# New places in SBUF for the split weight tiles of a decoder block: hi, lo and activation tiles all at 0 modulo 512 bytes

## The chip, the cores and the metric

The kernel runs on one core of one Trainium2 chip. The time is device microseconds (us) of one execution, the median of several runs. A nanosecond is written ns.

## The reference, cut to what matters

One decoder block on 256 tokens of 2048 float32 channels (depth 1): a combined input projection, a gated linear attention branch and a forgetting attention branch, their merge and output projection, LayerNorm, a gated MLP with a width-3 causal convolution, LayerNorm, and a gated embedding.

```python
proj = x @ w_in                                        # 2048 x 13336
y_gla = gla(...) @ w_branch_gla;  y_fox = fox(...) @ w_branch_fox
merged = sigmoid(ma) * y_gla + sigmoid(mb) * y_fox
x = layer_norm(ALPHA * x + merged @ w_out)
h = gelu(causal_dwconv(x @ w_gate)) * (x @ w_up)       # 2048 x 5632, twice
x = layer_norm(ALPHA * x + h @ w_down)                 # 5632 x 2048
x = x + sigmoid(x @ w_ple_gate) * (p @ w_ple_proj)
```

## The kernel before, in words

**Splitting.** All large products are made from float32r operands. Each weight chunk `raw` (128 partitions by 1024 float32) is loaded by a DMA, ScalarE (ACT) copies it to `hi` in float32r (L77, called from L101), and VectorE (DVE) writes `lo = raw - hi` (L103). Activations are split likewise and kept side by side: a tile such as `xT` or `x1T` has, for each of four k tiles, 256 columns of high part and 256 columns of low part.

**Units.** The weights come as 284 units of two chunks (`hi` and `lo` for each). `prep()` loads and splits one unit, `unit()` hands one out and keeps the preparation up to three units ahead.

**Weight-stationary products** (`w_unit`, L169 and L171): for each of the 16 k tiles of a unit one matmul with 128 columns of `hi` as stationary operand and the activation's 512 columns moving, and one with the same columns of `lo` and the activation's 256 high columns moving. These are the q, k, gate, up and branch products. I call the two matmuls a pair, and the eight pairs that use one `hi` tile and its `lo` tile a half-unit.

**Token-stationary products** (`x_mm`, L213): 128 columns of the activation are stationary and 512 columns of `hi` or `lo` move (v, r, the output projection `wo`, the down projection `dn`, the last gate `pg`, and `pp`, the embedding's projection, whose split weights `pw` and activations `pTs` both lie in tiles of the S8 pool).

**The first stage** (`fv`, L320) is token-stationary too, with rows of 1048 columns (`fvhi`, `fvlo`) cut in 352, 352 and 344 columns. After it, ACT copies its results out of PSUM (`smtok`, `fv`), TensorE (PE) transposes `smtok`, the gates are started (`gSt`, `psg` L396), and the first weight-stationary unit (`psfq`) follows.

**The core's other matmul groups** that the prediction names: `go` (L636), whose moving tile `vs` lies in the S8 pool and whose stationary tiles `ath`/`atl` lie in the pool of 2 KB scratch tiles.

**Places.** Tile pools give each tag a number of equal places in SBUF, as large as the tag's largest tile, and a tile takes a place at its first write. Before the change `hi` and `lo` share their tags with `fvhi` and `fvlo` (six places each, 1048 x 4 = 4192 bytes, so that the next place starts 96 bytes further modulo 512). The start of each tile per partition, modulo 512 bytes, as the built program has it:

| tiles | before | after |
|---|---|---|
| `hi`, six places | 32, 128, 224, 320, 416, 0 | 0 |
| the `lo` that goes with it | 96, 192, 288, 384, 480, 64 | 0 |
| S8 tiles (activations `xT`, `x1T`, `x2T`, `oT`, `ofT`, `mT`, `hT0` to `hT9`; `vs`, `pw`, `pTs`) | 160 | 0 |
| `hT10` | 416 | 128 |
| scratch tiles `ath`, `atl` | 160 | 384 |
| `fvhi`, `fvlo` | as `hi`, `lo` | 0 |

A k tile's 128 stationary columns are 512 bytes and an activation's k tile 2048 bytes, so steps inside a tile leave the value modulo 512 as it is, except in the first stage, whose chunks start 1408 and 2816 bytes into a row.

**What sets the order.** DMA issues on SyncE's queue (SP) stand in the program's order; the other engines' instructions are ordered by a scheduler when the program is built, which takes free places into account. In that order each engine's queue is strict.

Of the kernel before, what the change touches and what calls it, by code (L numbers as in the profile page):

```python
# [9 lines left out]
F32 = mybir.dt.float32  # L10
F32R = mybir.dt.float32r
# [8 lines left out]
P = 128  # L20
# [12 lines left out]
NS = 1048  # L33
# [4 lines left out]
AFF_DVE = (0, 2)  # L38
LN_ORDER = (1, 0, 3, 2)
GROWS = 96  # L40

OFF = dict(gq=0, gk=1024, gv=2048, gr=4096, glr=6144, fq=6160, fk=7184, fv=8208,
           ff=9232, ma=9240, mb=11288)
# [3 lines left out]
def tile_block(ctx: ExitStack, tc: tile.TileContext, wu, wfv, wpp, xT_in, x_in, pT_in, wlr,  # L47
# [1 line left out]
    nc = tc.nc  # L49

    cst = ctx.enter_context(tc.tile_pool(name="cst", bufs=1))
    ring = ctx.enter_context(tc.tile_pool(name="ring", bufs=6))
    big = ctx.enter_context(tc.tile_pool(name="big", bufs=15))
    sm = ctx.enter_context(tc.tile_pool(name="sm", bufs=2))
    early = ctx.enter_context(ExitStack())
    ec = early.enter_context(tc.tile_pool(name="ec", bufs=1))
# [1 line left out]
    pmx = ctx.enter_context(tc.tile_pool(name="pmx", bufs=2, space=PSUM))  # L58
    dr = ctx.enter_context(tc.tile_pool(name="dr", bufs=1, space=DRAM))

    def s8(shape, dt=F32, name=None):
        return big.tile(shape, dt, tag="S8", name=name)

    def t1(name):
        return sm.tile([P, 256], F32, tag="t1", bufs=6, name=name)
# [10 lines left out]
    def copy(o, i, scale=1.0):  # L76
        nc.scalar.activation(o, i, AF.Copy, bias=0.0, scale=scale)  # L77
# [15 lines left out]
    def prep():  # L93
        u = n_prep[0]
        n_prep[0] += 1
        his, los = [], []
        for h in range(2):
            raw = ring.tile([P, 1024], F32, tag="raw", bufs=4, name=f"raw{u}_{h}")
            nc.sync.dma_start(raw, wu[u, :, h * 1024:(h + 1) * 1024])
            hi = ring.tile([P, 1024], F32R, tag="hi", name=f"hi{u}_{h}")  # L100
            copy(hi, raw)  # L101
            lo = ring.tile([P, 1024], F32R, tag="lo", name=f"lo{u}_{h}")
            nc.vector.tensor_tensor(lo, raw, hi.bitcast(F32), ALU.subtract)  # L103
            his.append(hi)
            los.append(lo)
        ready[u] = (his, los)
# [4 lines left out]
    def unit():  # L111
        u = n_used[0]
        n_used[0] += 1
        while n_prep[0] < min(NU, u + 3):
            prep()
        return ready.pop(u)


    xT = [s8([P, 4, 512], F32R, name=f"xT{g}") for g in range(4)]

    def load_x(g, k0, k1, step=2):
# [6 lines left out]
                                    xT[g][:, e, 0:256].bitcast(F32), ALU.subtract)  # L128


    chn = cst.tile([P, chan.shape[1]], F32, name="chn")
    c_blr, c_bf = 0, 8
    c_g1, c_b1, c_g2, c_b2 = 9, 25, 41, 57
    c_cw = 73
    c_cb = c_cw + 3 * NF
    ident = cst.tile([P, P], F32, name="ident")
    mask = ec.tile([P, 8, 256], U8, name="mask")
    cmask = ec.tile([P, 256], F32, name="cmask")
    gnb = ec.tile([P, 512], F32, name="gnb")
    reset = ec.tile([P, 256], F32, name="reset")  # L140
    ones = ec.tile([P, P], F32R, name="ones")
    gSt = ec.tile([P, 256], F32R, name="gSt")
    mhalf = cst.tile([P, 1], F32, name="mhalf")
    nc.gpsimd.memset(mhalf, -0.5)
    nc.gpsimd.memset(reset, 1.0)
    copy(ones, reset[:, 1:2].broadcast_to([P, P]))
# [2 lines left out]
    def load_consts():  # L149
        nc.sync.dma_start(ident, ident_in)  # L150
        nc.sync.dma_start(chn, chan)
        nc.sync.dma_start(cmask, cmask_in)
# [128 lines left out]


    fv = s8([P, 2, 1024], name="fv")
    fch = ((0, 352), (352, 352), (704, 344))
    fbk = [[mmtile(f"fv_{t}{c}") for c in range(3)] for t in range(2)]

    def fv_prep(u, hs=(0, 1), his=None, los=None):
        his, los = his or [], los or []
        for h in hs:
            raw = ring.tile([P, NS], F32, tag="raw", bufs=4, name=f"fvraw{u}_{h}")  # L290
            hi = ring.tile([P, NS], F32R, tag="hi", name=f"fvhi{u}_{h}")
            lo = ring.tile([P, NS], F32R, tag="lo", name=f"fvlo{u}_{h}")
            for o, n in fch if u == 0 else ((0, NS),):
                e = slice(o, o + n)
                nc.sync.dma_start(raw[:, e], wfv[u, :, h, e])
                copy(hi[:, e], raw[:, e])
                nc.vector.tensor_tensor(lo[:, e], raw[:, e], hi[:, e].bitcast(F32), ALU.subtract)
            his.append(hi)
            los.append(lo)
        return his, los  # L300

    load_x(0, 0, 1, 1)
    f0 = fv_prep(0, (0,))
    load_x(0, 1, 2, 1)
    fvu = [fv_prep(0, (1,), *f0)]
    load_x(0, 2, 4)
    fvu.append(fv_prep(1))
    load_x(1, 0, 4)
    for u in range(8):
        hi, lo = fvu[u]  # L310
        for j in range(2):
            kt = 2 * u + j
            a = xT[kt // 4][:, kt % 4, :]
            for cs in ((0,), (1,), (2,)) if u == 0 else ((0, 1, 2),):
                for t in range(2):
                    ah, al = a[:, t * P:t * P + P], a[:, 256 + t * P:256 + t * P + P]
                    for i, (w, x) in enumerate(((hi[j], ah), (lo[j], ah), (hi[j], al))):
                        for c in cs:
                            o, n = fch[c]
# [9 lines left out]
        elif u == 4:  # L329
            load_consts()  # L330
    wraw = s8([GROWS, 1024], name="wraw")
    nc.gpsimd.memset(wraw, 0.0)
    for i in range(3):
        nc.sync.dma_start(wraw[32 * i:32 * i + 16], wlr)
    wS = s8([GROWS, 1024], F32R, name="wS")
    copy(wS, wraw)
# [3 lines left out]
    for t in range(2):  # L340
# [4 lines left out]
        copy(tk[:, P:P + FH], fbk[t][2][:, 336:344])  # L345
        nc.tensor.transpose(smp[:GROWS, t * P:t * P + P], tk[:, 0:GROWS], ident)
        nc.tensor.transpose(smp[:FH, 256 + t * P:256 + t * P + P], tk[:, P:P + FH], ident)
    for t in range(2):
        for c, (o, n) in enumerate(fch):
            n = min(n, 1024 - o)  # L350
# [4 lines left out]
    cd = dr.tile([FH, 256], F32, name="cd")  # L355
    gS = gSt[:GROWS]
    copy(gS, smp[:GROWS, 0:256])
    nc.vector.tensor_tensor(gS[32:48], smp[32:48, 0:256], gS[32:48].bitcast(F32), ALU.subtract)
# [137 lines left out]
    for nm, dst, sc in (("fq", fq, P ** -0.5), ("fk", fk, 1.0)):  # L496
        if nm == "fk":
            mixers.append(fox_gen())
        for n in range(8):
            hi, lo = unit()  # L500
# [8 lines left out]
    for nm, dst, sc in (("q", gq, 1.0 / 16.0), ("k", gk, 1.0)):  # L509
        for n in range(8):  # L510
            hi, lo = unit()
            ps = mmtile(f"ps{nm}{n}")
            w_unit(ps, hi, lo, xT, range(16), True, True)
            h, c = n // 2, n % 2
# [163 lines left out]
    for n in range(32):  # L678
        hi, lo = unit()
# [14 lines left out]
    for n in range(16):  # L694
        hi, lo = unit()
# [270 lines left out]
    for n in range(NF):  # L966
# [17 lines left out]
        u = t1("up")  # L984
# [140 lines left out]
```

## Time and profile before

| | |
|---|---|
| median of 3 runs | 1709.56 us (1709.23 to 1710.12) |
| span of the profiled execution, first to last instruction | 1706.3 us |
| PE busy, share of the span | 1698.7 us, 100% |
| DVE, ACT, POOL busy | 64%, 49%, 2% |
| DMA traffic | 330.22 MB, mean 194 GB/s |
| TensorE's granted clock | 1.00 |

The profiled execution is known by its span; the runs' median is 3.3 us longer, which is what lies around the first and last instruction. A matmul's row has its start, and a duration that includes the time until its last column has left the array; the next matmul starts earlier than that, so what one costs is read from the distance between starts (or from a piece of the chain of waits, which is counted from start to start), not from the duration. PEld is the weight load, which runs beside the matmul ahead of it. Of a view's columns, "x24" is the number of instructions in a row or group, and what stands in brackets is idle time before it and what ended it.

### The profile page before, as it was taken

To read this page: it belongs to the slowest core of one execution; us is meant where nothing else is said; L and a number is where in the kernel's file an instruction comes from. 1 tells how busy PE (TensorE), PEld (TensorE's weight loads), DVE (VectorE), ACT (ScalarE), POOL (GpSimd) and SP (SyncE) were. 2 spreads that over 40 slices of the span, in tenths; PEclk is the share of its full clock that TensorE was granted. 3 is DMA by queue.
4 is the path that set the end of the run, shared out by engine and by line. 5 is a ranking of instruction groups with operands and counts; after the bars stand their busy time and mean duration, and the time that the engine had idled before them with its cause. 6 is when DMAs were issued, how large, how long until landed. Compare 5 with 4: busy or idle time off the path is not lost.

```text
span 1706.3 us, 23834 instructions
## 1 busy us (share of the span) xinstructions
PE 1698.7 (100%) x9035; PEld 1456.3 (85%) x9035; DVE 1098.4 (64%) x1588; ACT 833.5 (49%) x1200; POOL 36.3 (2%) x123
## 2 busy tenths in 40 slices
PE   9999999999999999999999999999999999999998
PEld 8888888888888888888788888888888888888787
DVE  6666668758756557774687776666666644544674
ACT  5745445445555544443364444454445433334633
POOL 0000000000000000000010000000000000000000
PEclk9999999999999999999999999999999999999999
DMA  9754455555554555557655665555555575555454
GB/s 309 233 190 167 163 185 173 181 177 173 176 177 166 171 187 187 191 189 283 205 175 196 210 212 194 187 187 191 187 189 188 190 287 188 188 193 198 156 175 171
DMA packets 91427, 330.22 MB, mean 194 GB/s; under 512 B 10232, under 2 KB 11904, under 8 KB 89904
## 3 DMA queue, kind: packets, MB, share of 16 engines
q1 hardware_dynamic: 90528, 324.51, 56.1%
q0 software_dynamic: 784, 4.20, 0.7%
q8 instruction: 70, 1.15, 0.3%
q14 instruction: 45, 0.37, 0.1%
HBM read 323.42 MB, written 5.25 MB: 193 GB/s over the span
## 4 chain that ended last, share of the span: by engine, by line
PE 98%; DVE 1%; DMA 0%; ACT 0%; SPq 0%; issue 0%; POOL 0%
PE dn L213 14%; PE psu L169 9%; PE psg L169 9%; PE psm L169 7%; PE gr L213 5%; PE gv L213 5%; PE wo L213 5%; PE pg L213 5%; PE psu L171 5%; PE psg L171 5%; PE psm L171 4%; PE psa L169 3%; PE fv L320 2%; PE psa L171 2%; PE psfq L169 2%; PE psq L169 2%
## 5 line engine op out<-in xcount | busy, mean ns | idle before, releaser
L103 DVE TENSOR_TENSOR lo<-raw,hi 128x1024 fp32r<-128x1024 f32 x568 | 694.1, 1224 | 517.4 <-ACT hi L77 516.3
L77 ACT ACTIVATE hi<-raw 128x1024 fp32r<-128x1024 f32 x568 | 601.6, 1060 | 745.9 <-issue 277.2
L169 PE MATMUL psu<-x1T,hi 128*128 128x512 f32 x688 | 242.3, 393 | 0.0
L169 PE MATMUL psg<-x1T,hi 128*128 128x512 f32 x672 | 236.7, 393 | 0.0
L213 PE MATMUL dn<-hi,hT 128*128 128x512 f32 x704 | 193.2, 394 | 0.0
L171 PE MATMUL psu<-x1T,lo 128*128 128x256 f32 x688 | 192.8, 280 | 0.0
L171 PE MATMUL psg<-x1T,lo 128*128 128x256 f32 x672 | 188.4, 280 | 0.0
L169 PE MATMUL psm<-xT,hi 128*128 128x512 f32 x512 | 180.1, 395 | 0.0
L213 PEld LDWEIGHTS dn<-hi,hT 128*128 128x128 f32 x704 | 132.1, 188 | 30.9
L169 PEld LDWEIGHTS psu<-x1T,hi 128*128 128x128 f32 x688 | 129.1, 188 | 29.6
L169 PEld LDWEIGHTS psg<-x1T,hi 128*128 128x128 f32 x672 | 126.1, 188 | 28.9
L171 PE MATMUL psm<-xT,lo 128*128 128x256 f32 x512 | 143.3, 280 | 0.0
L171 PEld LDWEIGHTS psu<-x1T,lo 128*128 128x128 f32 x688 | 129.6, 188 | 0.0
L171 PEld LDWEIGHTS psg<-x1T,lo 128*128 128x128 f32 x672 | 126.6, 188 | 0.0
L169 PEld LDWEIGHTS psm<-xT,hi 128*128 128x128 f32 x512 | 96.3, 188 | 21.7
L213 PE MATMUL dn<-lo,hT 128*128 128x512 f32 x352 | 111.8, 395 | 0.0
L171 PEld LDWEIGHTS psm<-xT,lo 128*128 128x128 f32 x512 | 96.5, 188 | 0.2
L169 PE MATMUL psa<-oT,hi 128*128 128x512 f32 x256 | 90.1, 393 | 0.0
L213 PEld LDWEIGHTS dn<-lo,hT 128*128 128x128 f32 x352 | 66.1, 188 | 15.5
L213 PE MATMUL gv<-hi,xT 128*128 128x512 f32 x256 | 73.6, 399 | 0.0
L213 PE MATMUL gr<-hi,xT 128*128 128x512 f32 x256 | 73.5, 399 | 0.0
L213 PE MATMUL wo<-hi,mT 128*128 128x512 f32 x256 | 71.7, 395 | 0.0
(247 smaller groups left out, 2435.4 us busy)
## 6 DMA issues: line engine op xcount, KB each, us to landing
raw<-in_wu_dram SPq DMA_DIRECT2D x568, 512.0 KB, 3.6
fvraw<-in_wfv_dram SPq DMA_DIRECT2D x14, 524.0 KB, 6.3
lnb<-in_lng_dram SPq DMA_DIRECT2D x4, 1024.0 KB, 12.1
z<-in_x_dram SPq DMA_DIRECT2D x2, 1024.0 KB, 7.6
praw<-in_wpp_dram SPq DMA_DIRECT2D x4, 512.0 KB, 3.8
x1d<-z POOLq DMA_DIRECT2D x2, 1024.0 KB, 5.3
z<-x1d SPq DMA_DIRECT2D x2, 1024.0 KB, 7.6
xraw<-in_xT_dram SPq DMA_DIRECT2D x7, 256.0 KB, 7.1
```

Of the source, the lines that this page charges most:

```text
L77: nc.scalar.activation(o, i, AF.Copy, bias=0.0, scale=scale)
L103: nc.vector.tensor_tensor(lo, raw, hi.bitcast(F32), ALU.subtract)
L169: nc.tensor.matmul(ps, lhsT=hi[i // 8 if hoff == 0 else 0][:, w0 % 1024:w0 % 1024 + P], rhs=a[:, kt % 4, :], start=first and i == 0, stop= ...
L171: nc.tensor.matmul(ps[:, 256:512], lhsT=lo[i // 8 if hoff == 0 else 0][:, w0 % 1024:w0 % 1024 + P], rhs=a[:, kt % 4, 0:256], start=False, ...
L213: nc.tensor.matmul(bs[j][:, 0:m], lhsT=x, rhs=v[:, o:o + m], start=first and i == 0, stop=last and i == 2)
L320: nc.tensor.matmul(fbk[t][c][:, 0:n], lhsT=x, rhs=w[:, o:o + n], start=kt == 0 and i == 0, stop=kt == 15 and i == 2)
```

## The change

`hi` and `lo` get a pool of their own (`wide`) with places of 4096 bytes, laid out ahead of the others. `fvhi` and `fvlo` are no longer in the `hi` and `lo` rings but take tiles of the S8 pool (15 places), which `s8()` now always asks for at 2048 columns and cuts to shape. `raw` keeps four places of 4192 bytes. A tile `pad` of 88 columns and the moved constants bring the first place to 0 modulo 512. No instruction is added or taken away.

```diff
+PAD = 88
+S8W = 2048
+W4 = 1024
...
-    ring = ctx.enter_context(tc.tile_pool(name="ring", bufs=6))
+    wide = ctx.enter_context(tc.tile_pool(name="wide", bufs=6))
     big = ctx.enter_context(tc.tile_pool(name="big", bufs=15))
+    ring = ctx.enter_context(tc.tile_pool(name="ring", bufs=4))
...
+    pad = cst.tile([P, PAD], F32, name="pad")
...
     def s8(shape, dt=F32, name=None):
-        return big.tile(shape, dt, tag="S8", name=name)
+        t = big.tile([P, S8W], dt, tag="S8", name=name)
...
+    def w_tile(tag, dt, name):
+        return wide.tile([P, W4], dt, tag=tag, name=name)[:, 0:1024]
...
-            hi = ring.tile([P, 1024], F32R, tag="hi", name=f"hi{u}_{h}")
+            hi = w_tile("hi", F32R, f"hi{u}_{h}")
...
-            lo = ring.tile([P, 1024], F32R, tag="lo", name=f"lo{u}_{h}")
+            lo = w_tile("lo", F32R, f"lo{u}_{h}")
...
-            hi = ring.tile([P, NS], F32R, tag="hi", name=f"fvhi{u}_{h}")
-            lo = ring.tile([P, NS], F32R, tag="lo", name=f"fvlo{u}_{h}")
+            hi = s8([P, NS], F32R, name=f"fvhi{u}_{h}")
+            lo = s8([P, NS], F32R, name=f"fvlo{u}_{h}")
```

The order of instructions is the same on SP and POOL, and on the other engines everywhere but between the first stage and the first units. ACT at the end of the first stage, before (`wS` is a small split weight, `hi_0_622` and `hi_1_628` are the first unit's two chunks):

```order
L77 ACTIVATE wS<-wraw 96x1024
L77 ACTIVATE hi_0_622<-raw_0_620 128x1024
L77 ACTIVATE hi_1_628<-raw_1_626 128x1024
L77 ACTIVATE smtok<-fv_113 128x16
L77 ACTIVATE smtok<-fv_113 128x16 x2
L77 ACTIVATE smtok<-fv_113 128x8
L77 ACTIVATE fv<-fv_111 128x352
L77 ACTIVATE fv<-fv_112 128x352
```

ACT at the same place now, from the second token tile's copies on (`wS` stands seven rows ahead, right before the first `fv`; `hi_0_626` and `hi_1_632` are the first unit's chunks):

```order
L96 ACTIVATE fv<-fv_118 128x352
L96 ACTIVATE smtok<-fv_120 128x16
L96 ACTIVATE smtok<-fv_120 128x16 x2
L96 ACTIVATE smtok<-fv_120 128x8
L96 ACTIVATE fv<-fv_119 128x352
L96 ACTIVATE fv<-fv_120 128x320
L96 ACTIVATE gSt<-smp 96x256
L96 ACTIVATE hi_0_626<-raw_0_624 128x1024
L96 ACTIVATE hi_1_632<-raw_1_630 128x1024
```

The first unit's two copies have moved from ahead of the copies out of PSUM to behind them and behind `gSt`; the two subtractions on DVE that need them have moved behind `gSt` and `zf` likewise.

PE right after the last matmul of the first stage, before:

```order
L346 MATMUL smp<-ident,smtok 96x128 [waits DMAHW3_49,Activation_49,Pool_49]
L347 MATMUL smp<-ident,smtok 8x128 [waits Activation_49]
L169 MATMUL psfq_656<-xT_93,hi_0_622 128x512 [waits Activation_49]
L171 MATMUL psfq_656<-xT_93,lo_0_624 128x256 [waits DVE_49]
L346 MATMUL smp<-ident,smtok 96x128 [waits Activation_49,Pool_49]
L347 MATMUL smp<-ident,smtok 8x128 [waits Activation_49]
L169 MATMUL psfq_656<-xT_93,hi_0_622 128x512
```

And now:

```order
L362 MATMUL smp<-ident,smtok 96x128 [waits Activation_49,Pool_49]
L363 MATMUL smp<-ident,smtok 8x128 [waits Activation_49]
L412 MATMUL psg_696<-gSt,wS 128x256 [waits DVE_49]
L412 MATMUL psg_696<-gSt,wS 128x256
L412 MATMUL psg_760<-gSt,wS 128x256 [waits DVE_49,PE_49]
L185 MATMUL psfq_660<-xT_100,hi_0_626 128x512 [waits Activation_49]
L412 MATMUL psg_760<-gSt,wS 128x256
L187 MATMUL psfq_660<-xT_100,lo_0_628 128x256 [waits DVE_49]
```

Four of the gates' matmuls (`psg`) now stand ahead of the first unit, and the unit's first low-part matmul stands behind DVE's late subtraction. On POOL the order is the same, but the memset of `wraw`, which heads the small DMAs that stand on SP ahead of the first unit's loads, now takes over the place of `fvhi` of the sixth loading step and so waits for PE.

More of the change, by code (lines that the diff above doesn't have):

```diff
@@ L59, in tile_block @@
     dr = ctx.enter_context(tc.tile_pool(name="dr", bufs=1, space=DRAM))
+    chn = cst.tile([P, chan.shape[1]], F32, name="chn")
+    ident = cst.tile([P, P], F32, name="ident")
+    mhalf = cst.tile([P, 1], F32, name="mhalf")
+    pad = cst.tile([P, PAD], F32, name="pad")
     def s8(shape, dt=F32, name=None):
-        return big.tile(shape, dt, tag="S8", name=name)
+        t = big.tile([P, S8W], dt, tag="S8", name=name)
+        n = int(np.prod(shape[1:]))
+        t = t[:shape[0], :n]
+        if len(shape) == 3:
+            return t.rearrange("p (a b) -> p a b", b=shape[2])
+        if len(shape) == 4:
+            return t.rearrange("p (a b c) -> p a b c", b=shape[2], c=shape[3])
+        return t
+    def w_tile(tag, dt, name):
+        return wide.tile([P, W4], dt, tag=tag, name=name)[:, 0:1024]
     def t1(name):
@@ L128, in load_x @@
                                     xT[g][:, e, 0:256].bitcast(F32), ALU.subtract)
-    chn = cst.tile([P, chan.shape[1]], F32, name="chn")
     c_blr, c_bf = 0, 8
@@ L135, in tile_block @@
     c_cb = c_cw + 3 * NF
-    ident = cst.tile([P, P], F32, name="ident")
     mask = ec.tile([P, 8, 256], U8, name="mask")
@@ L142, in tile_block @@
     gSt = ec.tile([P, 256], F32R, name="gSt")
-    mhalf = cst.tile([P, 1], F32, name="mhalf")
     nc.gpsimd.memset(mhalf, -0.5)
```

## The prediction

> **What bounds the kernel now.** I read the page first: its span, and the chain that ended last.
>
> ```profile
> span 1706.3 us, 23834 instructions
> ...
> PE 98%; DVE 1%; DMA 0%; ACT 0%; SPq 0%; issue 0%; POOL 0%
> ```
>
> TensorE (PE) holds 98% of the chain, so a change counts only by what it does to the distance between the starts of PE's matmuls, or where it makes PE wait. Next I asked the stretch view for the whole span, for the high-part line L169, the low-part line L171 and the token-stationary line L213, one answer each.
>
> ```profile
> 0.00:1706.30 1706.30, 971.69 (x2768) 1.00 0.57 194
> ```
> ```profile
> 0.00:1706.30 1706.30, 775.30 (x2768) 1.00 0.57 194
> ```
> ```profile
> 0.00:1706.30 1706.30, 623.46 (x2688) 1.00 0.57 194
> ```
>
> There are 2768 pairs and 2688 token-stationary matmuls, at a granted clock of 1.00 throughout, so no clock is to be won. How far apart do matmuls of one shape start? The timeline of PE, in the middle of the gate and up products, at four of the seven starts of successive half-units (eight pairs each; the hi place of the first is 32, of the second 0, of the third 224, in bytes modulo 512):
>
> ```profile
> 1100.35 0.39 PE L169 MATMUL psg<-x1T,hi 128*128 128x512 f32 x1
> ...
> 1103.13 0.40 PE L169 MATMUL psg<-x1T,hi 128*128 128x512 f32 x1
> ...
> 1105.95 0.39 PE L169 MATMUL psu<-x1T,hi 128*128 128x512 f32 x1
> ...
> 1117.13 0.39 PE L169 MATMUL psu<-x1T,hi 128*128 128x512 f32 x1
> ```
>
> The reader is to see that equal work takes unequal time. The first half-unit took 2.78 us, 347.5 ns a pair; the second 2.82 us, 352.5 ns. PE waits for nobody there. What differs is the place of the stationary tile; the moving tile stays at 160. All six places together, 1100.35 to 1117.13, took 16.78 us for 48 pairs: **349.6 ns a pair** is what the mean place costs.
>
> The chain of waits, which counts from start to start, gives the 512-column matmuls of other stages:
>
> ```profile
> 13.25 39.55 PE fv L320 x246
> ...
> 252.71 5.59 PE gv L213 x24
> ...
> 496.85 2.05 PE go L636 x9
> ...
> 765.28 83.75 PE wo L213 x360
> ...
> 1357.72 239.31 PE dn L213 x1032
> ```
>
> `gv` takes 232.9 ns a matmul, `wo` 232.6, `dn` 231.9; here the stationary tile is at 160 and the moving one at the six places in turn. `go` takes 2.05 us for nine, **227.8 ns**, and it is the one group of the four whose moving and stationary tiles have the same place modulo 512 (160 and 160). That the equal place is the reason is my reading, not shown; it is the basis of the forecast. Two more groups have equal places, the embedding's projection `pp` in its two halves (two answers of the timeline):
>
> ```profile
> 857.34 3.01 PE L213 MATMUL pp<-pw,pTs 128*128 128x512 f32 x12
> ```
> ```profile
> 1604.54 1.75 PE L213 MATMUL pp<-pw,pTs 128*128 128x512 f32 x7
> ```
>
> A merged row ends with the last matmul's own 0.39 us. The later run: (1.75 - 0.39) / 6 = 226.7 ns a step. The earlier one, which stands between transposes: (3.01 - 0.39) / 11 = 238.2 ns, its first step included. So the equal place reaches the lowest value of the trace, but not after every interruption; I take 226.7 and 238.2 as the two ends for 512 columns.
>
> **The change part by part.**
>
> *Pairs.* All 2768 come to equal places, hi, lo and activation at 0. No row shows a pair of 512 and 256 columns at equal places. From below: one and a half times the `go` step, 341.7 ns, if 256 columns take half of 512. From above: the worst half-unit, 352.5. I take 343.5, near the lower end, because `go` is the nearest row (equal place, float32r, weights changed at every step); the 1.8 ns are for the steps after a wait, in which `pp` was slow. 2768 x (349.6 - 343.5) = **-16.9 us**; ends -21.9 and +8.0.
>
> *Token-stationary matmuls.* The 48 of `pp` have equal places already. The last four k tiles of `dn` read `hT10`, which lies at 128 now: 96 matmuls without a gain. 96 of the 2688 are of 256 columns; I count them with none. That leaves 2688 - 48 - 96 - 96 = 2448. They go from 232.2 (the mean of the three rows) to 228: 2448 x 4.2 = **-10.3 us**; ends from 226.7 and 238.2: -13.5 and +14.7.
>
> *First stage.* `fv` has 39.55 / 246 = 160.8 ns a step. The full `go` rate would give 227.8 x 352 / 512 = 156.6, but two of its three chunks start 384 and 256 bytes off the stationary tile's place. 288 matmuls, a third of them 4.2 ns faster: **-0.4 us**; ends -1.2 and +1.2.
>
> *Room.* A unit every 5.5 us instead of 5.6 asks little more of ACT and DVE, which are idle half and a third of the span. `fvhi` and `fvlo` rotate in the free S8 places, which is two and a half to three loading steps of 5.7 us ahead of PE, as in the rings before: nothing, ACT keeps its lead. `hi` and `lo` keep six places each, `raw` its four: the preparation keeps its lead in all later stages.
>
> *Hand-over from the first stage to the units.* The order shows the first unit's copies moved behind the copies out of PSUM and `gSt` on ACT. ACT, DVE and PE there, now:
>
> ```profile
> 43.61 1.06 ACT L77 ACTIVATE hi<-raw 128x1024 fp32r<-128x1024 f32 x1 [3.86 <-DMA raw<-in_wu_dram]
> ...
> 54.11 0.42 ACT L77 ACTIVATE gSt<-smp 96x256 fp32r<-96x256 f32 x1
> 54.37 2.04 ACT L77 ACTIVATE hi<-raw 128x1024 fp32r<-128x1024 f32 x2
> ```
> ```profile
> 54.56 0.42 DVE L358 TENSOR_TENSOR gSt<-smp,gSt 16x256 fp32r<-16x256 f32 x1 [6.97 <-ACT gSt L77]
> 55.01 0.47 DVE L363 TENSOR_SCALAR zf<-smp,chn 8x256 f32<-8x256 f32 x1
> 55.50 2.36 DVE L103 TENSOR_TENSOR lo<-raw,hi 128x1024 fp32r<-128x1024 f32 x2
> ```
> ```profile
> 52.77 0.47 PE L169 MATMUL psfq<-xT,hi 128*128 128x512 f32 x1
> ...
> 58.78 0.42 PE L396 MATMUL psg<-gSt,wS 96*128 96x256 f32 x2
> ```
>
> The first unit's copy is at 43.61, nine microseconds early. At 54.37 and 55.50 stand the second unit's copies and subtractions; after the change the first unit's will stand there. PE then gets its first low part at about 55.50 + 1.2 = 56.7 and needs 16 x 0.3435 - 0.23 = 5.3 us more for the unit: 62.0 instead of 58.78. Four `psg` matmuls, two groups of 0.25 us (the group at 58.78 is one), are done inside the wait. 62.0 - 58.8 - 0.5 = **+2.7 us**. Is the data there? The `wraw` memset now waits for the sixth loading step's first half:
>
> ```profile
> 37.79 1.11 PE L320 MATMUL fv<-fvhi,xT 128*128 128x352 f32 x6
> ```
> ```profile
> 1.55 0.96 POOL L332 MEMSET wraw<- 96x1024 f32 x1
> ```
> ```profile
> 32.61 1.35 SPq L334 DMA_DIRECT2D wraw<-in_wlr_dram  x3
> 34.00 0.42 SPq L155 DMA_DIRECT2D gnb<-in_gnorm_dram  x1
> 34.52 1.86 SPq L158 DMA_DIRECT2D maskf<-in_mask_dram  x2
> 38.18 38.82 SPq L99 DMA_DIRECT2D raw<-in_wu_dram  x17
> ```
>
> That half ends with the third of the six merged matmuls, at about 38.3, so the memset ends at about 39.3; behind it on SP queue `wraw` (1.35), `gnb` (0.42), `maskf` (1.86) and then the unit's loads, at about 42.9 instead of 38.18. The first load took 5.4 us, from 38.18 until ACT's 43.61: landed by 48.4, six microseconds ahead of ACT. So this wait is covered; without that cover it would cost what exceeds 54.4. Lower end of the hand-over 0 (the second unit's later copies are as far ahead as now, and the gates' matmuls move), upper end 7, if the four conversions that ACT and DVE still owe hold up the second and third unit too.
>
> Sum: -16.9 - 10.3 - 0.4 + 2.7 = **-24.9 us**: span 1706.3 to 1681.4, and, with the 3.3 us by which the runs' median exceeds the span, **1684.7 us**. Bounds of the terms: -36.6 and +30.9.
>
> *A rule against this change.* The half-units at 347.5 and 352.5 ns say that place matters. The Trainium skill, "TensorE: Matmul & The Clock Gate", Step-by-step: what each phase is for, says that PE has two independent read ports and that loading the next weights does not take read bandwidth from the running matmul; "SBUF — State Buffer", Who interferes with whom, says that PE never waits on anyone. By that rule the first three terms are nothing, and the sum is +2.7 us. The half-units disagree, as far as two equal runs of matmuls can.
>
> **The rivals.**
>
> *Place is not the cause* (the change doesn't do what it says): the half-units differ by something that rotates with them, and `go` is fast for another reason. For it: the earlier `pp` run at 238.2. Against: the half-units wait for nothing. Then only the hand-over is left: 1709.6 + 2.7 = 1712.3 us. Chance 8%. The skill's two ports, above, would give the same.
>
> *Equal places collide.* Weight load and matmul start together, so with equal places both ask for the same part of SBUF at the same moment, in every step instead of now and then. Place: all pairs and token-stationary matmuls. Price: pairs at the worst half-unit's 352.5, +8.0; token-stationary at the 238.2 of `pp`, +14.7; hand-over +2.7: 1709.6 + 25.4 = 1735.0 us. With the token-stationary matmuls unchanged at 232.2 it decides from 348.8 ns a pair (2.3 us of hand-over less first stage, over 2768), with them at 228 only from 352.5. For it: the hi place 0 half-unit is slow, and `pp` once. Against: `go` and the later `pp`. Chance 13%.
>
> *The gain is lost after every wait.* As in the earlier `pp` run, PE falls out of the fast step at each interruption, and comes back late: half of the first two terms, 1709.6 - 13.6 - 0.4 + 2.7 = 1698.3 us. Chance 12%.
>
> *More than the trace has seen.* No row shows both tiles at a multiple of 512; if that frees PE of more, the step falls below 226.7. With 5 ns less a 512-column step and 2.5 a 256-column one, 2768 x 7.5 + 2448 x 5 = 33 us more: about 1652 us. Chance 7%.
>
> **How the numbers follow.** The forecast, 1684.7, has the remaining 60%, and reaches from 1673 (all terms at their lower ends) to about 1695. A range from 1660 to 1713 takes in the forecast, the lost gain, the rival without effect and the nearer half of the larger gain, some 83%; the colliding places (13%) and the rest of the larger gain lie outside. About 0.2% (3.4 us) is what a measurement of this kernel can tell from no change. Faster by more: 60 + 12 + 7 = 79%. Within: the rival without effect, 1712.3, lies inside 1713.0, 7% with 1% of it beyond. Slower: 13 + 1 = 14%.
>
> **What would show it.** In the profile after: half-units of equal length, 2.75 us each, whichever place they use; `dn` near 228 ns a step up to its last 96; `go` no longer faster than the rest (its scratch tiles lie at 384 now, `vs` at 0); a wait of PE of some 4 us between 52 and 57 us that ends with DVE's `lo`. The forecast is wrong if half-units still differ among themselves, if pairs stay above 348 ns, or if the low-part matmul alone grows.

## The result, and the profile after

The changed kernel took 1710.86 us (1709.37 to 1712.4), beside 1709.26 us (1708.26 to 1710.16) of the kernel before on the same chip: ratio 1.0007, 95% interval 1.0 to 1.0015. That is no difference that can be measured; 1684.7 us was forecast. The page of the changed kernel, its span and its chain:

```profile
span 1707.1 us, 23843 instructions
...
PE 96%; DMA 1%; DVE 1%; ACT 1%; SPq 0%; issue 0%; POOL 0%; ACTq 0%
```

PE still sets the end. The page counts nine instructions more than before; all nine are semaphore instructions (seven on DVE, one each on POOL and SP), and matmuls, copies and transfers are as many as before. The time is the same as before, but not made up of the same parts. The starts of the stages, read from the timeline of PE in both profiled executions, give the length of each (us):

| from the first matmul of ... to that of the next | before | after | difference |
|---|---|---|---|
| the first stage to the first unit's last low part (`fv`, hand-over) | 54.01 | 57.10 | +3.09 |
| the remaining early units (`psfq` to `psk`, pairs) | 188.08 | 188.03 | -0.05 |
| `gv`, `gr` (token-stationary) | 192.16 | 188.37 | -3.79 |
| `psm`, `psa`, `psb` (pairs) | 326.21 | 329.60 | +3.39 |
| `wo`, `pp` (token-stationary) | 100.61 | 99.40 | -1.21 |
| `psg`, `psu` (gate and up, pairs) | 491.83 | 497.27 | +5.44 |
| `dn` (token-stationary) | 253.58 | 248.71 | -4.87 |
| `pg` (token-stationary), to its last matmul | 90.57 | 89.40 | -1.17 |

The token-stationary products won 11.0 us, and the pairs lost 8.8 us where 16.9 us were to be won. The first stage and hand-over lost 3.1; 0.5 of that are the gates' four `psg` matmuls, two groups of 0.25 us, which stood behind the first unit before. The sum is +0.8 us, the difference of the spans.

**The token-stationary side** is seen in the chain of waits of the changed kernel, from start to start:

```profile
13.68 37.37 PE fv L336 x235
249.94 5.50 PE gv L229 x24
496.07 2.09 PE go L652 x9
813.65 36.80 PE wo L229 x161
1364.57 234.43 PE dn L229 x1032
```

`dn` stands at 234.43 / 1032 = 227.2 ns a step, where it stood at 231.9; `wo` at 228.6. `go`, whose tiles now lie apart, is the slow one: 232.2 ns instead of 227.8. Fast and slow have changed places as the tiles have. The same shows inside `dn`: the last four k tiles of each half of the output read `hT10`, at 128 now. The timeline of PE, ahead of the first such stretch and in it:

```profile
1466.02 1.07 PE L229 MATMUL dn<-hi,hT 128*128 128x512 f32 x4
...
1472.82 1.09 PE L229 MATMUL dn<-hi,hT 128*128 128x512 f32 x4
...
1474.22 1.09 PE L229 MATMUL dn<-hi,hT 128*128 128x512 f32 x4
...
1482.58 1.10 PE L229 MATMUL dn<-hi,hT 128*128 128x512 f32 x4
```

Thirty matmuls take 6.80 us ahead of it, 226.7 ns each; 36 matmuls in it take 8.36 us, 232.2 ns each. Behind it `dn` is back at 226.7. In one stage of one run the fast step goes and comes back with the equal place.

**The pairs** are seen in the gate and up products. Two answers on the tile `psu`, before and after (least, median and greatest duration in ns, then the first and the last start in us; between them lie 1360 pairs, 688 of `psu` and 672 of `psg`):

```profile
L169 PE MATMUL psu<-x1T,hi x688: 387/392/398, 882.3 to 1357.2; 128*128 128x512 f32 x172
L171 PE MATMUL psu<-x1T,lo x688: 278/280/285, 882.5 to 1357.4; 128*128 128x256 f32 x172
```
```profile
L185 PE MATMUL psu<-x1T,hi x688: 395/398/403, 883.9 to 1364.1; 128*128 128x512 f32 x172
L187 PE MATMUL psu<-x1T,lo x688: 277/281/284, 884.1 to 1364.3; 128*128 128x256 f32 x172
```

From the first high part to the end of the last low part (some 0.12 us behind its start): 475.2 us before, 349.4 ns a pair; 480.5 us after, **353.3 ns** a pair. The low part's duration is as it was. The high part's grew by 6 ns, and its least duration after (395) lies above the median before. The half-units are of equal length now, as forecast, but long. PE's timeline at three successive third high parts, and at the starts of two half-units:

```profile
1095.88 0.40 PE L185 MATMUL psg<-x1T,hi 128*128 128x512 f32 x1
...
1096.94 0.40 PE L185 MATMUL psg<-x1T,hi 128*128 128x512 f32 x1
...
1098.00 0.40 PE L185 MATMUL psg<-x1T,hi 128*128 128x512 f32 x1
...
1098.71 0.40 PE L185 MATMUL psu<-x1T,hi 128*128 128x512 f32 x1
...
1101.53 0.40 PE L185 MATMUL psu<-x1T,hi 128*128 128x512 f32 x1
```

Three pairs take 1.06 us, again and again, and a half-unit 2.82 or 2.83 us. But the same places can do better. In the first two units behind the hand-over, three pairs took 1.04 us, 346.7 ns each; here the second:

```profile
62.56 0.39 PE L185 MATMUL psfq<-xT,hi 128*128 128x512 f32 x1
...
63.60 0.39 PE L185 MATMUL psfq<-xT,hi 128*128 128x512 f32 x1
```

In the higher cycle the three pairs differ (350, 361 and 349 ns from start to start); in the lower one they are alike. So my first theory (A) was that at equal places a pair has two steady cycles, 346.7 and 353.3 ns, and that the turn from 512 to 256 columns and back makes both longer than 227 + 113 ns. Against it stood B, that the low part's equal place is what costs, and C, that something beside PE that came with the new layout slows it.

### The profile page after: what moved, and what is told of

It reads as the page before. It is cut to its first block, busy times and chain, and to the rows that moved or that the text cites. A ratio compares the mean times of both kernels' runs of the same rounds, so it can differ in the third digit from the quotient of the medians.

```text
span 1707.1 us, 23843 instructions
## 1 busy us (share of the span) xinstructions
PE 1697.0 (99%) x9035; PEld 1455.9 (85%) x9035; DVE 1098.3 (64%) x1588; ACT 833.9 (49%) x1200; POOL 37.8 (2%) x123
## 4 chain that ended last, share of the span: by engine, by line
PE 96%; DMA 1%; DVE 1%; ACT 1%; SPq 0%; issue 0%; POOL 0%; ACTq 0%
PE dn L229 14%; PE psu L185 9%; PE psg L185 9%; PE psm L185 7%; PE gv L229 5%; PE gr L229 5%; PE psu L187 5%; PE pg L229 5%; PE psg L187 5%; PE psm L187 4%; PE psa L185 4%; PE wo L229 3%; PE fv L336 2%; PE psa L187 2%; PE psb L185 2%; PE psk L185 2%
## 5 line engine op out<-in xcount | busy, mean ns | idle before, releaser
L187 PE MATMUL psa<-oT,lo 128*128 128x256 f32 x256 | 71.9, 281 | 0.0
```

The costliest lines, as they stand in the source:

```text
L187: nc.tensor.matmul(ps[:, 256:512], lhsT=lo[i // 8 if hoff == 0 else 0][:, w0 % 1024:w0 % 1024 + P], rhs=a[:, kt % 4, 0:256], start=False, ...
```

## The experiments

The table gives all twelve runs beside the kernel before of the same chip. "Pair" is worked out from the answer on `psu` as above, "dn" from the chain's piece of 1032.

| run | us | ratio to before, 95% | pair, ns | dn, ns |
|---|---|---|---|---|
| before | 1709.26 | | 349.4 | 231.9 |
| after | 1710.86 | 1.0 to 1.0015 | 353.3 | 227.2 |
| e1, 8 high, 8 low | 1700.20 | 0.9928 to 0.9953 | 349.1 | 227.1 |
| e2, the same on before | 1712.65 | 1.0006 to 1.0024 | 351.4 | 231.9 |
| e3, lo at 256 | 1711.07 | 0.9998 to 1.0016 | 353.3 | 227.2 |
| e4, seven splits | 1706.29 | 0.9972 to 0.9992 | 350.2 | 227.1 |
| e5, 8 and 8, lo at 448 | 1704.93 | 0.9964 to 0.9985 | 348.0 | 231.1 |
| e6, lo at 448 | 1705.70 | 0.9963 to 0.9983 | 346.7 | 231.1 |
| e7, activations at 160 | 1709.06 | 0.9988 to 1.0006 | 346.7 | 233.3 |
| e8, wraw elsewhere | 1707.13 | 0.9983 to 1.0 | 353.4 | 227.2 |
| e9, e8 and two splits | 1703.82 | 0.9960 to 0.9982 | 353.3 | 227.2 |
| e10, 2 high, 2 low | 1699.33 | 0.9927 to 0.9954 | 348.3 | 227.1 |
| e11, e9, unit 5 | 1695.36 | 0.9906 to 0.9933 | 347.4 | 227.1 |
| e12, e9, unit 3 | 1703.60 | 0.9951 to 0.9978 | 353.3 | 227.1 |

**e1 and e2: the order within a half-unit.** In `w_unit`, on the changed kernel and on the one before:

```diff
-        for i, kt in enumerate(kts):
...
+        for i0 in range(0, n, 8):
+            for part in (0, 1):
+                for i in range(i0, min(n, i0 + 8)):
+                    kt = kts[i]
...
+                    w = (hi, lo)[part][i // 8 if hoff == 0 else 0][:, w0 % 1024:w0 % 1024 + P]
+                    if part == 0:
...
```

> The changed kernel, with the eight high-part matmuls of a half-unit ahead of its eight low-part matmuls instead of in turn; the same matmuls, places and number. Theory A (alternation): at equal places matmuls of one shape follow each other at the low step that dn shows after the change (227 ns for 512 columns, so about 113 for 256), and it is the turn from 512 to 256 columns and back that costs 7 or 13 ns a pair, in one of two steady cycles (347 and 353 ns a pair in the trace after). Then a pair falls to (8 x 227 + 8 x 113.5 + one turn of 7 to 13) / 8 = 341 to 342 ns, 2768 x (353.7 - 341.5) = 34 us less: about 1677 us. Theory B (place of lo): the low part at the moving tile's own place is what costs. Then the low steps stay at 117 ns or above in their runs, a pair is 227 + 117 = 344 or more: 1684 us or more. Theory C (something that comes with the new places beside PE, such as the writes of ACT, DVE and the DMAs): the order changes nothing, 1711 us.

> The kernel before (places spread modulo 512), with the same order of eight high parts and eight low parts. Theory A, with place deciding what a run of one shape costs: the high parts go at what token-stationary matmuls cost before, 232.2 ns in the mean of the places, the low parts at about half, 116; a pair is about 348.5 to 349, and the time 1704 to 1709 us, a small gain or none. If the order alone is worth it, whatever the places: as the changed kernel in this order, about 1677 us. Theory C says nothing changes, 1709 us.

In e1 PE's timeline merges each run of eight:

```profile
1095.28 2.00 PE L190 MATMUL psu<-x1T,hi 128*128 128x512 f32 x8
1097.12 1.11 PE L193 MATMUL psu<-x1T,lo 128*128 128x256 f32 x8
1098.07 2.00 PE L190 MATMUL psg<-x1T,hi 128*128 128x512 f32 x8
```

Eight high parts take 1.84 us, 230 ns each, and eight low parts 0.95 us, 119 ns. So C falls: order alone changes the time at the same places. A is half wrong: the pair came to 349.1 ns, not 341.5, since low parts at equal places go at 119 ns for as long as they follow each other. B is still open here, as it had the low steps at 117 ns or above and the pair above 344. On the kernel before, the same order lost: 351.4 ns, where 348.5 to 349 were expected. So what e1 wins over the kernel before is the token-stationary gain, with pairs that are no dearer than they were.

**e3 and e6: lo elsewhere.** A pool of its own for `lo`, and pads so that `hi` and activations stay at 0:

```diff
-        return wide.tile([P, W4], dt, tag=tag, name=name)[:, 0:1024]
+        return (wlo if tag == "lo" else wide).tile([P, W4], dt, tag=tag, name=name)[:, 0:1024]
```

> The changed kernel with all lo tiles 256 bytes further, at 256 modulo 512, while hi and activations stay at 0; order in turn as it was. Theory A: a pair stays between the two cycles, 346.5 to 353.5 ns, and may fall into the other one: 1690 to 1711 us, and the low step stays above 113. Theory B: the low step falls to 113 to 114 and the pair to 344 or less: 1684 us or less. Theory C: 1711 us.

> The same places (hi and activations at 0, lo at 448), but high and low parts in turn as in the changed kernel. If the place of lo alone is what was missing: low steps at 113, a pair near 341 to 344, 1685 to 1694 us. If the turn itself costs (two cycles of 347 and 353 ns whatever the place): a pair of 346.5 to 353.5, and with 0 to 11 us lost in the token-stationary products 1692 to 1722 us.

The high parts of `psu` in e3 and in e6:

```profile
L191 PE MATMUL psu<-x1T,hi x688: 395/398/403, 886.1 to 1366.3; 128*128 128x512 f32 x172
```
```profile
L191 PE MATMUL psu<-x1T,hi x688: 391/396/396, 887.0 to 1358.1; 128*128 128x512 f32 x172
```

480.2 us in e3, 471.1 in e6, from the first high part to the last, for 1359 pairs: 353.3 and 346.7 ns, the same two values as with equal places. B falls: neither place of `lo` brought a pair below the lower cycle. In e6 the low steps did go to 113 ns, and the high parts to 233 in exchange. `dn` shows the other side: 227.2 ns with `lo` 256 bytes off, 231.1 with it 64 bytes off (at 448).

**e5: low runs at the place that had looked best.**

> The changed kernel with eight high parts ahead of eight low parts, and all lo tiles at 448 modulo 512 while hi and activations stay at 0. In the run with eight and eight on the kernel before, the low-part steps whose moving place less stationary place was 64 settled at 113 to 114 ns, in no other relation in the mean below 117; with equal places they settled at 120. Theory A2 (each shape has its own best relation of places, and the low part's is not the equal one): low steps at 113.3, high parts as in the run with equal places (1841 ns for eight), a pair (1841 + 8 x 113.5) / 8 = 343.6 ns, 2768 x (349.1 - 343.6) = 15 us less than with equal places in runs. Against it stand the token-stationary products, a third of whose matmuls now move a tile at 448 past activations at 0: 0 to 11 us of their gain is lost. Time 1685 to 1696 us. Rival (256 columns cannot go below 117 to 120 for long, whatever the place): 1700 us or more.

```profile
1098.21 1.11 PE L199 MATMUL psu<-x1T,lo 128*128 128x256 f32 x8
```

Its low steps took (1.11 - 0.28) / 7 = 118.6 ns, and 117.1 in the runs whose row has 1.10 us, not 113.5; `dn` gave 4 ns back. Theory A2 fails. In e2, runs of low parts with the very same relation of places had gone at 113 ns:

```profile
1105.36 1.07 PE L177 MATMUL psg<-x1T,lo 128*128 128x256 f32 x8
```

(1.07 - 0.28) / 7 = 112.9 ns. One relation of places, two steady steps: place does not settle it alone, for runs of one shape either.

**e7: is the equal place what the token-stationary products gained from?** A pad of 160 bytes ahead of the S8 pool; the pools behind it move along.

> The changed kernel with the activations' pool 160 bytes further (activations at 160, where they were before, hi and lo at 0). If the equal place is what brought the token-stationary products to 227.5 ns, dn goes back to 230 to 236 ns a step, and the 11 us that these products had won are lost: together with pairs at 346.5 to 353.5 ns, 1702 to 1722 us. If it was the distance of 4096 bytes between places, or another side of the new layout: dn stays at 227.5.

The chain of e7, and its high parts of `psu`:

```profile
1357.95 240.81 PE dn L231 x1032
```
```profile
L187 PE MATMUL psu<-x1T,hi x688: 388/392/400, 886.3 to 1357.4; 128*128 128x512 f32 x172
```

240.81 / 1032 = 233.3 ns: the gain is gone, though `hi` and `lo` still lie 4096 bytes apart. The relation of the two places was the cause there. It need not be the equal one: e3, with a third of the moving tiles 256 bytes off, kept 227.2. And the pairs, at unequal places, went at 346.7 ns. Whether that comes of these places or of what went before, e7 can't say: no split was tried in this layout.

**e8: the hand-over undone.**

```diff
-    wraw = s8([GROWS, 1024], name="wraw")
+    wraw = ring.tile([GROWS, 1024], F32, tag="raw", bufs=4, name="wraw")
```

> The changed kernel with wraw in the raw ring instead of a place of the S8 pool, so that its memset no longer waits for the first stage; the order of ACT then has the first unit's two copies ahead of the copies out of PSUM again. The hand-over term, +2.7 us, should go: the first unit's last matmul where it was before, and 1708.2 us, if the pairs stay in the cycles that they are in. A change of the moment at which PE starts the units may also put other stages into the other cycle, a few us either way.

PE at the first unit, in the changed kernel and in e8:

```profile
54.69 0.95 PE L412 MATMUL psg<-gSt,wS 96*128 96x256 f32 x3 [0.97 <-DVE gSt L374]
55.48 0.40 PE L185 MATMUL psfq<-xT,hi 128*128 128x512 f32 x1
...
56.43 0.39 PE L187 MATMUL psfq<-xT,lo 128*128 128x256 f32 x1 [0.43 <-DVE lo L122]
```
```profile
52.44 0.47 PE L185 MATMUL psfq<-xT,hi 128*128 128x512 f32 x1
...
55.34 0.40 PE L185 MATMUL psfq<-xT,hi 128*128 128x512 f32 x1
...
56.40 0.40 PE L185 MATMUL psfq<-xT,hi 128*128 128x512 f32 x1
...
57.46 0.40 PE L185 MATMUL psfq<-xT,hi 128*128 128x512 f32 x1
```

The first unit starts at 52.44 instead of 55.48, and its last low part 3.35 us earlier; by the two ratios (1.0007 and 0.9991) the time fell by 2.7 us, though their intervals meet at 1.0; the profiled spans differ by 2.1 us. Here the first unit stands in the 1.06 us cycle, where the changed kernel's first two stand in that of 1.04 us: same places, same matmuls, another start.

**e4, e9, e11 and e12: throwing PE from one cycle into the other.** The last three start from e8. One high-part matmul of a unit, the first of its second half, is given as two of 256 columns; the places stay as they are, and so does what is computed.

```diff
+            if split and i == 8:
+                for c in range(2):
+                    nc.tensor.matmul(ps[:, 256 * c:256 * c + 256], lhsT=w,
+                                     rhs=a[:, kt % 4, 256 * c:256 * c + 256],
+                                     start=False, stop=False)
```

> The changed kernel with one high-part matmul of 512 columns given as two of 256 in seven of the up product's units (every sixth), otherwise unchanged. Theory A with two steady cycles: PE keeps the cycle it is in until something breaks the turn; in the gate and up products, which go at 353.4 ns a pair from end to end, single splits should now and then throw it into the 347 cycle, where it then stays until the next split. Time between 1700 and 1712 us. If the step depends on places alone (theories B and C), every split costs at most 0.1 us on the spot, and 353.4 ns holds on both sides of each: 1711 to 1712 us.

PE around the first split (L188), and around the second:

```profile
929.00 0.40 PE L192 MATMUL psu<-x1T,hi 128*128 128x512 f32 x1
...
931.12 0.40 PE L192 MATMUL psu<-x1T,hi 128*128 128x512 f32 x1
...
931.82 0.40 PE L188 MATMUL psu<-x1T,hi 128*128 128x256 f32 x2
...
932.89 0.39 PE L192 MATMUL psu<-x1T,hi 128*128 128x512 f32 x1
...
934.97 0.39 PE L192 MATMUL psg<-x1T,hi 128*128 128x512 f32 x1
...
990.09 0.39 PE L192 MATMUL psg<-x1T,hi 128*128 128x512 f32 x1
...
995.64 0.39 PE L192 MATMUL psu<-x1T,hi 128*128 128x512 f32 x1
...
998.41 0.40 PE L188 MATMUL psu<-x1T,hi 128*128 128x256 f32 x2
...
1001.23 0.40 PE L192 MATMUL psg<-x1T,hi 128*128 128x512 f32 x1
...
1006.88 0.40 PE L192 MATMUL psu<-x1T,hi 128*128 128x512 f32 x1
```

Ahead of the first split six pairs take 2.12 us (353 ns each), behind it 2.08 (347). PE stays there for eleven units, 5.55 us each, until the second split throws it back: the unit from 1001.23 takes 5.65 us. All seven splits changed the cycle, four down and three up. One split matmul in twelve units, at the same places, moved the pair by 6.7 ns for all that followed: A's two cycles are shown.

> The changed kernel with wraw in the raw ring (no hand-over wait) and two single splits of a high-part matmul into two of 256 columns: one in the merge gates' unit 24, behind the last attention matmuls, and one in the up product's unit 4. Theory (two steady cycles, a pair at 346.7 or 353.3 ns, kept until something breaks the turn): both splits meet PE in the 353.3 cycle, as in the trace of the run with wraw alone, and throw it into the other, where it stays through the merge gates and the branch products (some 500 pairs, 3.4 us) and through the gate and up products (some 1340 pairs, 8.9 us): 1707.1 - 12.3 = 1694.8 us, 1692 to 1698. Rival (the cycle is drawn anew or comes back by itself): 1700 to 1707 us.

The first split did what was expected: the merge gates and branch products went from 353.3 to 346.7 ns. The one in `psu` unit 4 did nothing, so that the time, 1703.82 us, lies outside the 1692 to 1698 expected and where the rival had it; but in the trace no cycle changes by itself in a steady stretch. Units in the higher cycle take 353.1, 353.8 and 353.1 ns a pair in turn, because 16 pairs are no multiple of three; unit 4 stood at another point than the splits of e4.

> As the run with two splits, but the second split in the up product's unit 5 instead of unit 4. The 353.3 cycle repeats after three pairs and a unit has 16, so successive units stand at three different points of it; a unit of 353.8 ns a pair stands once in every three. The split of unit 4, behind a unit of 353.1, changed nothing, all four that threw PE into the lower cycle stood behind a unit of 353.8, and unit 5 stands behind such a one. If the point of the cycle decides: 346.7 ns a pair from unit 5 to the end of the gate and up products, some 1330 pairs, 8.8 us less than the run with two splits: 1695 us, 1693 to 1697. If it is chance, or unit 4 failed for another reason (too early in the stage): 1704 us.

> The same with the second split in unit 3, which stands at the third point of the cycle (behind a unit of 353.1 that follows one of 353.8). If the point of the cycle decides, every split at this point does the same: either as unit 5 (1695 us) or as unit 4 (1704 us); the theory doesn't say which. 346.7 from there on would show that unit 4 was not too early in the stage.

PE in e11, by starts of units, and the high parts of `psu` in e12:

```profile
917.52 0.40 PE L192 MATMUL psg<-x1T,hi 128*128 128x512 f32 x1
...
923.18 0.40 PE L192 MATMUL psu<-x1T,hi 128*128 128x512 f32 x1
...
928.80 0.39 PE L192 MATMUL psg<-x1T,hi 128*128 128x512 f32 x1
...
934.35 0.39 PE L192 MATMUL psu<-x1T,hi 128*128 128x512 f32 x1
```
```profile
L192 PE MATMUL psu<-x1T,hi x687: 395/398/403, 878.9 to 1359.1; 128*128 128x512 f32 x172
```

In e11 a unit takes 5.66 us ahead of the split and 5.55 behind it, to the end of the products: 1695.36 us, as expected to 0.4 us, and the best of all runs, ahead of both kernels. Unit 3 did as unit 4: 480.2 us for 1359 pairs. (The expectation describes the point of unit 4; unit 3 stands behind the second of two units of 353.1. The three units still stand at three different points.) So in the gate and up products a split changes the higher cycle at one of its three points and not at the other two, in the places tried.

**e10: shorter runs.** As e1 with two and two.

> The changed kernel with two high parts ahead of two low parts, everything else as changed. If it is each turn between 512 and 256 columns that costs a fixed 6.7 to 13.3 ns a pair in steady cycles, half as many turns cost half: a pair of 343.3 to 346.7 ns, 1682 to 1692 us. If what settles is a level that does not go below 346.7 ns whatever the order, as the run with eight and eight (349.1 ns a pair) suggests: 346.7 to 353.4 ns, 1692 to 1712 us.

From 882.5 to 1356.1 us in the answer on `psu`, 348.3 ns a pair: the second of the two theories. Half as many turns do not cost half. Theory A's price by the turn is given up; what stands of A is that steady levels exist, and that no order tried here went below 346.7 ns in a steady stretch of pairs.

## Why the prediction was wrong

**The pairs: the step that failed.** "I take 343.5, near the lower end, because `go` is the nearest row." At equal places the pairs settled at 353.3 ns in most of `psm` and all of `psa` to `psu`, just outside the upper end of 352.5, and only at times at 346.7. The term was forecast at -16.9 us and measured +8.8. The lower end was wrong as well: one and a half `go` steps, 341.7, scaled a run of one shape to a sequence of two, and the low part does not scale so (119 ns in e1, where half of 227 is 113.5). Had every pair gone at the lower cycle, the term would have been 2768 x (346.7 - 349.6) = -8.0 us, half of what was forecast.

**What "place" does.** The forecast took the time as a function of the place. The splits show that the same places leave two steady cycles open, and that an interruption can throw PE from one into the other. With all places equal PE stays where the last interruption left it: in the gate and up products for 1360 pairs in the higher cycle. That it did not stay so before the change because each half-unit brought other places is my reading, not shown. Of my rivals, "the gain is lost after every wait" had something of this, a fast step lost at an interruption, but for half the gain of all products; the token-stationary matmuls kept theirs, and the pairs lost more than theirs. "Equal places collide" had the direction at the pairs, and nearly its price (352.5).

**The total.** 1710.86 us lies inside the range of 1660 to 1713 and near the 1712.3 of the rival without effect. That is chance: the token-stationary gain of 11.0 us was used up by 8.8 on the pairs and 3.1 at the hand-over. Of the signs that were named as speaking against the forecast, pairs above 348 ns came.

**Token-stationary.** Right, in cause and size: -11.0 us against -10.3. `go` became slow as forecast, and e7 took the gain away by moving the activations. `dn` is slow where it was to be, but in two stretches of 48, not in its last 96. The Trainium skill, "TensorE: Matmul & The Clock Gate", Step-by-step: what each phase is for, says of the two read ports that loading weights takes no read bandwidth from the running matmul. By it e7 would have left `dn` at 227.2 ns; it went to 233.3, so the measurement decides against a reading of that rule as "place costs nothing". Whether it is the ports that meet, no run here shows.

**First stage and hand-over.** Forecast +2.7 and -0.4. The first unit started 2.71 us later than before and e8 took that back. The form was otherwise: not one wait of 4 us, but three of 0.34, 0.97 and 0.43 us on `smp`, `gSt` and `lo`, with `psg` matmuls between. `fv` ended 0.03 us earlier, not 0.4: its step fell from 160.8 to 159.0 ns (37.37 / 235), but its one wait, on ACT's `fvhi`, grew from 0.3 to 0.7 us. The cover that was counted on held: the unit's loads were issued at 42.38 us (42.9 in the working), and ACT reached the copies at 54.04.

**Room.** Nothing, as forecast: PE's waits in the later stages stayed below 0.3 us each but for those that were there before.

**What stays open:** why the cycles have these lengths, what at the start of a stage picks one (the changed kernel, e3 and e8 took the higher one in the gate and up products, e6 and e7 the lower, so that the places may lean to one), whether the higher cycle exists at all in the layouts of e6 and e7, and whether a pair can go below 346.7 ns.

## What to carry to other kernels

A step that repeats thousands of times can have more than one steady length at the same places; read it from start to start on both sides of an interruption before giving a layout its price. Take as the best case the lowest value that the trace shows for the very sequence (here a half-unit of two shapes), not one scaled from another sequence. Where the trace shows two lengths for equal work at equal places, a single irregular matmul at the right point can be worth as much as a new layout: the change of places alone won nothing, and e11, which has the new places and two such matmuls, won 0.8% (0.9906 to 0.9933). The second of them is worth some 8.5 us, the step from e9 to e11.

## What the runs showed of the hardware

- Pairs of 512 and 256 columns at equal places keep one of two steady cycles for up to 1360 pairs: 346.7 ns a pair, every pair alike, or three pairs in 1.06 us (353.3 ns a pair). The lower value came up with lo at 448 and with activations at 160 too, the higher with lo at 256. One matmul given as two switched the cycle at the same places (e4: seven of seven; e9 and e12: the second not).
- `dn` took 227.2 ns a step with moving and stationary tile at the same place modulo 512, and as much with a third of the moving tiles 256 bytes off (e3); 231.1 with a third of them 64 bytes off (e5, e6), and 233.3 with all 160 off (e7). In the changed kernel it took 226.7 at equal places and 232.2 where the stationary tile lay 128 bytes off.
- Eight low parts in a row went at 113 ns (e2) and at 117 to 119 ns (e5) with the same relation of places.
